# A hybrid block with 32 streamed experts: three experts kept on chip at the end, the first expert's bias loaded apart

## The chip, the cores and the metric

The kernel runs on one core of one Trainium2 chip. Its time is the device time of one execution in microseconds (us). Before the change it was 1566.69 us, the median of three runs (1562.38 to 1566.81). All data is float32.

## The reference

The block has one layer and 512 tokens of 1024 values. A mixer comes first (two kinds of recurrent heads); its result is added to x. Then comes the part that this change touches: a norm, a router, a mixture of 32 experts of which each token uses four, and a last norm.

```
h = modulate(rms_norm(x, norm_ffn), sh2, sc2)
logits = h @ w_router + b_router
top_logit, top_idx = top_k(logits, 4);  top_w = softmax(top_logit)
# for each expert e, the rows h[tok] of the tokens that chose it:
gu   = h[tok] @ w_gate_up[e] + b_gate_up[e]              # 1024 -> 2048
gate = minimum(gu[:, :1024], 7);  up = clip(gu[:, 1024:], -7, 7)
act  = (up + 1) * gate * sigmoid(1.702 * gate)
y    = act @ w_down[e] + b_down[e]                       # 1024 -> 1024
x    = x + g2 * sum over a token's four experts of top_w * y
out  = modulate(rms_norm(x, norm_final), sh_f, sc_f)
```

## The kernel before

The first 470 us are the mixer and the router. The router counts each expert's tokens and orders the experts on the chip by a table (ORDER gives, for a position in the program, the rank by number of tokens of the expert that is computed there; position 0 is always expert 0, the real one, since its weights are loaded before the order is known). In the following "expert n" is the n-th position.

**Weights.** An expert's weights are 12 MB: eight loads of 1 MB for gate_up ("gu", 128 rows of 2048 values each) and four for down ("wd"), all issued by SP. They go into 1 MB buffers, called `wst` in the profile, of which there are twenty; `fill` issues the next load (line 107) in a fixed list as soon as a buffer is free, so the loads follow each other as fast as buffers come free. `weights` (lines 1640 to 1649) writes that list: down of expert n-1 behind gate_up of n, and for the last two each expert's own down behind its gate_up.

**Rows.** Tokens go through an expert in groups of 32. UNITS_OF gives for every position how many groups are always computed and how many at most; the groups between stand under a branch on the expert's count. One group through one load is `up32`: four matmuls whose 32-column results lie side by side in U (groups 0 and 1) or E (groups 2 and 3). In the trace one float32 matmul leaves two records, so one group through one load is eight. The rows of an expert are gathered from the DRAM buffer xd (`gather`, POOL), transposed (`turn`, DVE), multiplied with gate_up, activated (`act`, DVE and ACT), multiplied with down, and written to a DRAM buffer yd (`send`, POOL). The bias enters U and E as a matmul of 8 rows (`add_bias`, line 1668) that opens the accumulation; `load_bias` brings it, POOL issuing the DMA.

**The first expert.** Its rows are not gathered: `first_rows` (line 1286) picks them by matmuls with a selection matrix P and ACT copies them (line 1288). In `up(0)` the first four loads serve groups 0 and 1 first; then every load serves the groups left, and is freed.

**The end.** Behind expert 29 stands `overflow`, a branch for counts that exceed the plan; in front of it all outstanding work is waited for. Then come experts 30 and 31, the two with the fewest tokens, of one group each. Expert 30's rows are kept on chip in Yb (line 1808). `fetch(k)` (lines 2062 and 2065) brings, for each token, the row of its k-th expert back from yd, in four indirect DMAs of 512 KB into the buffers yk, and DVE adds it to x: four fetches, 8 MB. `late_prep` builds selection matrices; `late_add` (lines 2094 and 2095) adds expert 30's kept rows by matmuls and DVE adds; `norm_all` takes the last norm; `late_rows` and `late_end` handle the tokens of expert 31, whose rows are computed last and written over the output by one scatter (line 2145).

The buffers of the end come from the same twenty (`last_slots`): yk takes two and other tables two, for which four are held in reserve; x and two more buffers of the kernel take four, and twelve carry the last loads.

Of the kernel before, what the change touches and what calls it, by code (L numbers as in the profile page):

```python
# [22 lines left out]
ORDER = [(0, 1, 1, 1, 0), (1, 5, 1, -1, 29), (5, 16, 5, 1, 1), (18, 19, 1, 1, 4), (21, 30, 2, 1, 5), (22, 29, 2, -1, 13), (6, 10, 1, -1, 25), (11, 15, 1, -1, 21), (16, 18, 1, -1, 17), (19, 21, 1, -1, 15), (30, 32, 1, -1, 31)]  # L23
# [4 lines left out]
UNITS_OF = [[(4, 4), (4, 6), (3, 4), (2, 3), (2, 2), (1, 2), (1, 1)][sum(r >= k for k in (1, 5, 10, 16, 26, 30))] for r in RANK]  # L28
# [651 lines left out]
class Mixer(Base):  # L680
# [598 lines left out]
    def first_rows(s, P, h):  # L1279

        p = s.b2([128, 4, 128], name="px")
        for k in range(4):
            for b in range(4):
                for q in range(4):
                    c = 256 * q + 32 * (4 * h + k)
                    s.nc.tensor.matmul(p[32 * q:32 * q + 32, k], s.h2s[b // 2][:, b % 2, c:c + 32], P[:, b], start=b == 0, stop=b == 3)
        for i, t in enumerate((s.xT[:, 0], s.xTx[:, 0:2])):
            s.nc.scalar.copy(t[:, :, 4 * h:4 * h + 4], p[:, :, 64 * i:64 * i + 64].rearrange("p k (u t) -> p u k t", u=2))
# [9 lines left out]
    def front(s):  # L1298
# [3 lines left out]
        c = s.fc  # L1302
        with s.tc.tile_pool(name="psf", bufs=1, space=PSUM) as ps:
# [47 lines left out]
            for b in range(4):  # L1351
                s.pump()
                ms = s.sm([128, 2], name="ms2")
                xT = []
                if b:
                    p = s.mix_mm(0, Y, lambda: xT.extend(s.x_T(b - 1, n) for n in range(2)))
                    pl = s.logits(xT)
                    del xT
                else:
                    Y1 = []  # L1360
                    p, p1 = s.mix_first(Y, lambda: Y1.extend(s.mix_T(1)))
                s.mix_add(b, 0, p, ms)
                if 0 < b < 3:
                    Y1 = s.mix_T(b + 1)
                p = s.mix_mm(1, Y) if b else p1
                if b == 3:
                    s.free(8)
                    s.fill()
                if b:
                    s.top4(b - 1, pl, prev)  # L1370
                s.mix_add(b, 1, p, ms)
                if b < 3:
                    Y = Y1
                else:
                    pl = s.logits([s.x_T(3, n) for n in range(2)])
                if b == 2:
                    s.free(2)
                if b == 0:
                    scale2()
                rs = s.norm2(ms)  # L1380
                if b % 2 == 0:
                    s.h2s.append(s.slot([128, 2, 1024], name="h2"))
                h2 = s.h2s[-1][:, b % 2]
                for n in range(2):
                    s.h2_rows(b, rs, h2, n, g if n or b < 3 else v)
                s.h2_out(b, h2, g)
                g.dma_start(s.xd[:, b], s.x[b])
                if b < 2:
                    s.heads_out(b + 2)
                if b == 1:  # L1390
                    s.free(2)
                    s.split_bias()
                if b < 3:
                    s.fill()
                prev = rs
            del Y, Y1, p
            s.top4(3, pl, rs)
# [20 lines left out]
class Block(Mixer):  # L1418
# [25 lines left out]
    def lists(s):  # L1444
# [18 lines left out]
        s.first_rows(s.P, 0)  # L1463
# [16 lines left out]
    def routing(s):  # L1480
# [19 lines left out]
        s.first_rows(s.P, 1)  # L1500
        del s.P
# [31 lines left out]
    def weights(s):  # L1533
# [56 lines left out]
        s.wl = c.tile([128, 4, 2], F32, name="wl")  # L1590
        v.tensor_copy(s.wl, s.pw[:, :, 30:32])
        late = s.sm([128, 4, 2], name="late")
        v.tensor_scalar(late, s.pos[:, :, 30:32], 32.0, None, op0=ALU.is_ge)
        v.tensor_mul(row[:, :, 30:32], row[:, :, 30:32], late)
        v.tensor_mul(s.pw[:, :, 30:32], s.pw[:, :, 30:32], late)
# [25 lines left out]
    def moe_weights(s):  # L1621
# [21 lines left out]
        for n in range(2, 30):  # L1643
            load_up(n)
            load_down(n - 1)
        load_down(29)
        for n in (30, 31):
            load_up(n)
            load_down(n)
# [16 lines left out]

    def add_bias(s, U, bias):
        s.nc.tensor.matmul(U, s.B8, bias, start=True, stop=False)  # L1668
# [68 lines left out]
    def up(s, e, mid=None):  # L1737
# [14 lines left out]
        if e == 0:  # L1752
            W = [s.get(("gu", 0, kk)) for kk in range(4)]
            for kk in range(4):
                for u in range(2):
                    s.up32(W[kk], xs[u], outs[u], kk)
            for kk in range(8):
                w = W[kk] if kk < 4 else s.get(("gu", 0, kk))
                for u in range(2 if kk < 4 else 0, 4):
                    s.up32(w, xs[u], outs[u], kk)  # L1760
                done()
                if kk == 3:
                    mid()
# [30 lines left out]
    def down_last(s, e):  # L1794
# [10 lines left out]
        if e == 30:  # L1805
# [47 lines left out]
    def moe(s):  # L1853
        nc = s.nc
        engs = [ET.PE, ET.Activation, ET.DVE]
        s.bias, s.c = {}, {}
        todo = s.weights()
        s.bias[0] = s.load_bias(0)
# [16 lines left out]
        for e in range(1, 31):  # L1875
            for u in range(2):
                s.gather(s.XG[:, (e + 1) % 2, u], s.idx[:, u, e + 1:e + 2])
            s.gather_more(e + 1)
            s.bias[e + 1] = s.load_bias(e + 1)
            if e == 28:  # L1880
                s.reserve = 3
            if e == 29:
# [3 lines left out]
            if e == 30:  # L1886
                s.last_slots()
                s.reserve = 0
                s.overflow()
                s.Yb = s.B1[:, 1]  # L1890
                nc.gpsimd.memset(s.Yb, 0.0)
                s.up(30)
                s.turn(31)
                s.down_last(30)
                for k in range(4):
                    s.fetch(k)
                s.late_prep()
                s.up(31)
                s.late_add()
                s.norm_all()  # L1900
                s.late_rows()
                break
# [6 lines left out]
            if e == 29:  # L1909
                s.down(29)  # L1910
                s.bias_down()
# [5 lines left out]
            if e == 3:  # L1917
                for u in range(2, 6):
                    s.index(u, s.y([128, 32], "y"))
        s.late_end(s.down_last(31))  # L1920
# [138 lines left out]
    def fetch(s, k):  # L2059

        for b in range(4):
            s.nc.gpsimd.indirect_dma_start(s.yk[b], None, s.yd[0:ROWA[30]],  # L2062
                                           bass.IndirectOffsetOnAxis(ap=s.rid[:, b, k:k + 1], axis=0))
        for b in range(4):
            s.nc.vector.scalar_tensor_tensor(s.x[b], s.yk[b], s.wk4[:, b, k:k + 1], s.x[b], op0=ALU.mult, op1=ALU.add)  # L2065

    def late_prep(s):
# [3 lines left out]
        tf, q5 = s.sm([128, 2], name="tf"), s.sm([128, 1], name="q5")  # L2071
        v.tensor_scalar(q5, s.qoff, -4096.0, None, op0=ALU.add)
        v.tensor_copy(tf, s.idx[:, 0, 30:32])
        v.tensor_scalar(tf, tf, q5, None, op0=ALU.subtract)
        v.tensor_scalar(s.PT, s.io5, tf[:, 0:1], None, op0=ALU.is_equal)  # L2075
# [3 lines left out]
        v.tensor_scalar(f, tf[:, 1:2], 4.0, None, op0=ALU.mult)  # L2079
# [8 lines left out]
    def late_add(s):  # L2088

        for b in range(4):  # L2090
            for n in range(2):
# [3 lines left out]
                s.nc.vector.scalar_tensor_tensor(s.x[b][:, ns], p, s.wl[:, b, 0:1], s.x[b][:, ns], op0=ALU.mult, op1=ALU.add)  # L2095
# [17 lines left out]
    def late_rows(s):  # L2113
# [8 lines left out]
        for b in range(4):  # L2122
            for j in range(4):
                te.matmul(w[32 * j:32 * j + 32, :], s.P1[:, b], s.wl[:, b, 1:2], start=b == 0, stop=b == 3)
# [60 lines left out]
```

## Time and profile before

| | |
|---|---|
| median of three runs | 1566.69 us (1562.38 to 1566.81) |
| the profiled execution | 1567.19 us |
| its span | 1565.6 us |
| PE busy | 1304.7 us, 83% |
| DVE, POOL, ACT busy | 549.2, 370.4, 180.5 us |
| read from HBM | 487.82 MB |
| mean rate of the span | 332 GB/s |

The profile is of one execution. Its span reaches from the first to the last instruction; the profiled execution's own time is 1.6 us longer. A line of the timeline is one instruction, or several alike that follow each other (x8), with its start, its length and, in brackets, how long its engine had been idle before and what released it. "SPq" is SP issuing DMAs. [...] The DMA share is the mean busy share of the core's 16 DMA engines; it can pass 1 by rounding.

### The profile page before, as it was taken

To read this page: it belongs to the slowest core of one execution; us is meant where nothing else is said; L and a number is where in the kernel's file an instruction comes from. 1 tells how busy PE (TensorE), PEld (TensorE's weight loads), DVE (VectorE), ACT (ScalarE), POOL (GpSimd) and SP (SyncE) were. 2 spreads that over 40 slices of the span, in tenths; PEclk is the share of its full clock that TensorE was granted. 3 is DMA by queue.
4 is the path that set the end of the run, shared out by engine and by line. 5 is a ranking of instruction groups with operands and counts; after the bars stand their busy time and mean duration, and the time that the engine had idled before them with its cause. 6 is when DMAs were issued, how large, how long until landed. Compare 5 with 4: busy or idle time off the path is not lost. (4 is left out here: it accounts for less than half of the span.)

```text
span 1565.6 us, 31529 instructions
## 1 busy us (share of the span) xinstructions
PE 1304.7 (83%) x13085; PEld 659.4 (42%) x13085; DVE 549.2 (35%) x1221; ACT 180.5 (12%) x366; POOL 370.4 (24%) x601
## 2 busy tenths in 40 slices
PE   5878978999978777899789978999898898887623
PEld 4656657967762322243224322434333342333201
DVE  6455552465753371332121212113111321112256
ACT  3433412144220000000000000000000000000001
POOL 2212234340221322021302130231222122212230
PEclk9989989969988886999999999999999999998757
DMA  9933535745186799999999999999999999999881
GB/s 303 331 114 135 206 131 156 293 183 165 44 346 268 297 415 415 417 417 417 417 419 417 417 418 417 417 413 417 414 416 411 414 416 412 415 410 393 323 361 56
DMA packets 135351, 518.40 MB, mean 331 GB/s; under 512 B 26454, under 2 KB 49642, under 8 KB 99338
## 3 DMA queue, kind: packets, MB, share of 16 engines
q1 hardware_dynamic: 108794, 465.68, 74.6%
q0 software_dynamic: 18960, 47.38, 7.9%
q10 hardware_dynamic: 7424, 2.89, 0.7%
q8 instruction: 126, 2.06, 0.5%
q14 instruction: 47, 0.39, 0.1%
HBM read 487.82 MB, written 32.51 MB: 332 GB/s over the span
## 5 line engine op out<-in xcount | busy, mean ns | idle before, releaser
L1674 PE MATMUL U<-wst,B 128*32 128x512 f32 x3712 | 449.6, 618 | 58.3 <-DMA wst<-in_w_gate_up 47.0
L1674 PEld LDWEIGHTS U<-wst,B 128*32 128x32 f32 x3712 | 117.8, 112 | 359.2 <-issue 245.3
L1696 PE MATMUL y<-wst,B 128*32 128x256 f32 x3712 | 221.6, 391 | 41.7 <-DMA wst<-in_w_down 28.6
L1706 POOL DMA_DIRECT2D yd<-ys x160 | 85.8, 542 | 604.2 <-DVE ys L1701 373.8
L1681 DVE TENSOR_SCALAR ag<-U 128x512 f32<-128x512 f32 (+1 forms) x32 | 20.5, 640 | 545.5 <-PE U L1674 519.1
L1696 PEld LDWEIGHTS y<-wst,B 128*32 128x32 f32 x3712 | 130.5, 112 | 144.6 <-DMA wst<-in_w_down 38.4
L1674 PE MATMUL E<-wst,B 128*32 128x512 f32 x1152 | 145.3, 614 | 9.4 <-DVE au L1683 9.4
L1682 ACT ACTIVATE as<-ag 128x512 f32<-128x512 f32 (+1 forms) x45 | 25.4, 564 | 972.4 <-DVE ag L1681 972.4
L532 POOL TENSOR_TENSOR lo<-wst,hi 128x1024 fp32r<-128x1024 f32 x30 | 74.8, 2512 | 156.3 <-ACT hi L531 154.5
L1520 POOL DMA_INDIRECT B<-xd,idx x62 | 65.9, 1063 | 109.8 <-DMA yd<-ys 41.3
L1701 DVE TENSOR_TENSOR ys<-y,g2j 128x256 f32<-128x256 f32 x72 | 30.5, 424 | 145.0 <-PE y L1696 132.1
L1674 PEld LDWEIGHTS E<-wst,B 128*32 128x32 f32 x1152 | 39.3, 113 | 98.9 <-issue 86.8
L1696 PE MATMUL y<-wst,h 128*32 128x256 f32 x1152 | 64.9, 380 | 1.8 <-DVE ys L1701 0.8
L573 PE MATMUL pu<-hi,hh 128*128 128x256 f32 x192 | 57.0, 297 | 6.0 <-DVE tmz L664 4.5
L574 PE MATMUL pu<-lo,hh 128*128 128x256 f32 x192 | 55.4, 289 | 0.0
L575 PE MATMUL pu<-hi,hl 128*128 128x256 f32 x192 | 55.1, 287 | 0.0
L628 DVE SCALAR_TENSOR_TENSOR cva<-cvt,tap,cva 128x511 f32<-128x511 f32 (+2 forms) x48 | 41.9, 879 | 24.6 <-ACT cva L625 23.3
L558 PE MATMUL pu<-hh,hi 128*128 128x512 f32 x96 | 41.5, 432 | 10.0 <-ACT cva L625 10.0
L1696 PEld LDWEIGHTS y<-wst,h 128*32 128x32 f32 x1152 | 36.9, 110 | 29.8 <-DVE ys L1701 7.3
L573 PEld LDWEIGHTS pu<-hi,hh 128*128 128x128 f32 x192 | 37.6, 196 | 10.8 <-DVE tmz L664 4.9
L1668 PE MATMUL U<-bias,B 8*128 8x512 f32 x58 | 23.0, 469 | 21.6 <-PEq L1719 8.4
L559 PE MATMUL pu<-hl,hi 128*128 128x512 f32 x96 | 39.3, 410 | 0.0
(545 smaller groups left out, 1524.3 us busy)
## 6 DMA issues: line engine op xcount, KB each, us to landing
wst<-in_w_gate_up SPq DMA_DIRECT2D x256, 1024.0 KB
wst<-in_w_down SPq DMA_DIRECT2D x128, 1024.0 KB
wst<-in_w_ada SPq DMA_DIRECT2D x24, 1024.0 KB
wst<-in_w_in SPq DMA_DIRECT2D x14, 1024.0 KB
yd<-zero POOLq DMA_DIRECT2D x7, 2048.0 KB, 22.7
wst<-in_w_ada_final SPq DMA_DIRECT2D x8, 1024.0 KB
yd<-ys POOLq DMA_DIRECT2D x124, 64.0 KB, 6.0
x<-in_x SPq DMA_DIRECT2D x8, 512.0 KB
```

Source lines behind the costliest of these rows:

```text
L532: (engs or (nc.gpsimd, nc.gpsimd))[n].tensor_sub(lo[:, a], w[:, a], hi[:, a].bitcast(F32))
L558: te.matmul(p[:, ct, :], hi[:, kk, cs], hx, start=kk == 0, stop=False)
L559: te.matmul(p[:, ct, :], hi[:, kk, cs], lx, start=False, stop=False)
L573: te.matmul(p[:, b, :], hx, hi[:, kk, :], start=kk == 0, stop=False)
L574: te.matmul(p[:, b, :], hx, lo[:, kk, :], start=False, stop=False)
L575: te.matmul(p[:, b, :], lx, hi[:, kk, :], start=False, stop=kk == 7)
L628: v.scalar_tensor_tensor(a[:, d:], th[:, :512 - d], w[j], a[:, d:], op0=ALU.mult, op1=ALU.add)
L1520: s.nc.gpsimd.indirect_dma_start(dst, None, s.xd4.rearrange("q t c -> (q t) c"), bass.IndirectOffsetOnAxis(ap=idx, axis=0), bounds_check=2 ...
L1674: s.nc.tensor.matmul(U[32 * j:32 * j + 32, :], x[:, kk, :], w[:, :, j, :], start=False, stop=kk == 7)
L1696: s.nc.tensor.matmul(y[32 * j:32 * j + 32, :], a[:, kt, :], W[:, kt % 2, 256 * j:256 * j + 256], start=start, stop=kt == 7)
L1701: s.nc.vector.tensor_mul(t, y, s.g2j)
L1706: s.nc.gpsimd.dma_start(rows.rearrange("(u t) c -> t u c", t=32)[:, :, 256 * j:256 * j + 256], t[32 * j:32 * j + 32])
```

## The change

Three positions are of the lightest kind, 29, 30 and 31 (one group each, where one more was possible at 29); the others move up by one position, with expert 4 of a smaller size. The branch `overflow` stands one expert sooner, behind expert 28. Experts 29 and 30 are both kept on chip and added by `late_add`; only 31 is still scattered. `fetch` is cut in two, DMA issue and adds, and the parts stand between the stages of the last three experts. For an expert of one group, one gather is issued in place of two.

At the start, `bias0` loads expert 0's bias as plain float32 into a place of its own, issued before the lists are made; `up(0)` puts all four groups through each load. `top4` of the third token block stands before that block's `h2_rows`, and `first_rows` is interrupted after two of its four column blocks so that the matmul of the order (pperm) comes between.

```diff
...
-UNITS_OF = [[(4, 4), (4, 6), (3, 4), (2, 3), (2, 2), (1, 2), (1, 1)][sum(r >= k for k in (1, 5, 10, 16, 26, 30))] for r in RANK]
+UNITS_OF = [[(4, 4), (4, 6), (3, 4), (2, 3), (2, 2), (1, 2), (1, 1)][sum(r >= k for k in (1, 5, 10, 16, 26, 29))] for r in RANK]
...
                 for q in range(4):
                     c = 256 * q + 32 * (4 * h + k)
                     s.nc.tensor.matmul(p[32 * q:32 * q + 32, k], s.h2s[b // 2][:, b % 2, c:c + 32], P[:, b], start=b == 0, stop=b == 3)
+            if k == 1:
+                yield
         for i, t in enumerate((s.xT[:, 0], s.xTx[:, 0:2])):
             s.nc.scalar.copy(t[:, :, 4 * h:4 * h + 4], p[:, :, 64 * i:64 * i + 64].rearrange("p k (u t) -> p u k t", u=2))
 
...
                 if b % 2 == 0:
                     s.h2s.append(s.slot([128, 2, 1024], name="h2"))
                 h2 = s.h2s[-1][:, b % 2]
+                if b == 3:
+                    s.top4(3, pl, rs)
                 for n in range(2):
                     s.h2_rows(b, rs, h2, n, g if n or b < 3 else v)
                 s.h2_out(b, h2, g)
...
                     s.fill()
                 prev = rs
             del Y, Y1, p
-            s.top4(3, pl, rs)
+            s.bias0()
             s.lists()
             s.free(2)
             s.fill()
...
         s.P = s.t2([128, 4, 128], name="P")
         for b in range(4):
             nc.vector.tensor_scalar(s.P[:, b], s.io, 1.0, pos[:, b:b + 1], op0=ALU.add, op1=ALU.is_equal)
-        s.first_rows(s.P, 0)
+        s.first = s.first_rows(s.P, 0)
+        next(s.first)
 
     def rounds(s, a, b):
...
         load_up(0)
         load_down(0)
         load_up(1)
-        for n in range(2, 30):
+        for n in range(2, 29):
             load_up(n)
             load_down(n - 1)
-        load_down(29)
-        for n in (30, 31):
+        load_down(28)
+        for n in (29, 30, 31):
             load_up(n)
             load_down(n)
 
...
         s.nc.gpsimd.dma_start(t.bitcast(F32), s.bgD[:, bass.ds(e, 1), :].rearrange("j o c -> j (o c)"))
         return t
 
+    def bias0(s):
+
+        t = s.B1[0:8, 1, 512:1024]
+        s.nc.gpsimd.dma_start(t, s.bgD[:, 0:1, :].rearrange("j o c -> j (o c)"))
+        s.bias = {0: t}
+
     def add_bias(s, U, bias):
-        s.nc.tensor.matmul(U, s.B8, bias, start=True, stop=False)
+        s.nc.tensor.matmul(U, s.B8 if bias.dtype == F32R else s.B8.bitcast(F32), bias, start=True, stop=False)
 
     def up32(s, W, x, U, kk):
 
...
             s.free(n)
             s.fill()
         if e == 0:
-            W = [s.get(("gu", 0, kk)) for kk in range(4)]
-            for kk in range(4):
-                for u in range(2):
-                    s.up32(W[kk], xs[u], outs[u], kk)
             for kk in range(8):
-                w = W[kk] if kk < 4 else s.get(("gu", 0, kk))
-                for u in range(2 if kk < 4 else 0, 4):
+                w = s.get(("gu", 0, kk))
+                for u in range(4):
                     s.up32(w, xs[u], outs[u], kk)
                 done()
                 if kk == 3:
...
                 w = None
                 s.free()
                 s.fill()
-        if e == 30:
+        if e < 31:
...
         s.up(0, mid)
         s.turn(1)
         s.c[1] = s.count(1, engs)
-        for e in range(1, 31):
-            for u in range(2):
-                s.gather(s.XG[:, (e + 1) % 2, u], s.idx[:, u, e + 1:e + 2])
-            s.gather_more(e + 1)
-            s.bias[e + 1] = s.load_bias(e + 1)
+
+        def ahead(e):
+            for u in range(min(UNITS_OF[e][1], 2)):
+                s.gather(s.XG[:, e % 2, u], s.idx[:, u, e:e + 1])
+            s.gather_more(e)
+            s.bias[e] = s.load_bias(e)
+        for e in range(1, 29):
+            ahead(e + 1)
+            if e == 27:
+                s.reserve = 3
             if e == 28:
-                s.reserve = 3
-            if e == 29:
                 s.load_xd()
                 s.bdown()
                 s.reserve = 4
-            if e == 30:
-                s.last_slots()
-                s.reserve = 0
-                s.overflow()
-                s.Yb = s.B1[:, 1]
-                nc.gpsimd.memset(s.Yb, 0.0)
-                s.up(30)
-                s.turn(31)
-                s.down_last(30)
-                for k in range(4):
-                    s.fetch(k)
-                s.late_prep()
-                s.up(31)
-                s.late_add()
-                s.norm_all()
-                s.late_rows()
-                break
             s.up(e)
             s.turn(e + 1)
             s.turn_more(e + 1)
             if UNITS_OF[e + 1][1] > UNITS_OF[e + 1][0]:
                 s.c[e + 1] = s.count(e + 1, engs)
             s.down(e - 1)
-            if e == 29:
-                s.down(29)
-                s.bias_down()
             next(todo, None)
             if e == 1:
                 s.rounds(8, 16)
...
             if e == 3:
                 for u in range(2, 6):
                     s.index(u, s.y([128, 32], "y"))
+        s.down(28)
+        s.bias_down()
+        ahead(30)
+        s.last_slots()
+        s.reserve = 0
+        s.overflow()
+        s.Yb = s.B1[:, 1]
+        nc.gpsimd.memset(s.Yb, 0.0)
+        got = [s.fetch(k) for k in range(4)]
+        next(got[0])
+        s.up(29)
+        s.turn(30)
+        ahead(31)
+        s.down_last(29)
+        s.late_prep()
+        s.late_add(29)
+        next(got[0], None)
+        next(got[1])
+        s.up(30)
+        s.turn(31)
+        next(got[1], None)
+        next(got[2])
+        s.down_last(30)
+        s.late_add(30)
+        next(got[2], None)
+        next(got[3])
+        s.up(31)
+        next(got[3], None)
+        s.norm_all()
+        s.late_rows()
         s.late_end(s.down_last(31))
 
     def overflow(s):
...
     def fetch(s, k):
 
         for b in range(4):
-            s.nc.gpsimd.indirect_dma_start(s.yk[b], None, s.yd[0:ROWA[30]],
+            s.nc.gpsimd.indirect_dma_start(s.yk[b], None, s.yd[0:ROWA[29]],
                                            bass.IndirectOffsetOnAxis(ap=s.rid[:, b, k:k + 1], axis=0))
+        yield
         for b in range(4):
             s.nc.vector.scalar_tensor_tensor(s.x[b], s.yk[b], s.wk4[:, b, k:k + 1], s.x[b], op0=ALU.mult, op1=ALU.add)
 
...
                 r = slice(32 * j, 32 * j + 32)
                 nc.gpsimd.tensor_copy(s.sj[r, h], s.B3[r, h, 256 * j:256 * j + 256])
 
-    def late_add(s):
-
+    def late_add(s, e):
+
+        s.nc.vector.tensor_scalar(s.PT, s.io5, s.tf[:, e - 29:e - 28], None, op0=ALU.is_equal)
         for b in range(4):
             for n in range(2):
                 p = s.y([128, 512], "y")
                 ns = slice(512 * n, 512 * n + 512)
                 s.nc.tensor.matmul(p, s.PT[:, 128 * b:128 * b + 128], s.Yb[:, ns], start=True, stop=True)
-                s.nc.vector.scalar_tensor_tensor(s.x[b][:, ns], p, s.wl[:, b, 0:1], s.x[b][:, ns], op0=ALU.mult, op1=ALU.add)
+                s.nc.vector.scalar_tensor_tensor(s.x[b][:, ns], p, s.wl[:, b, e - 29:e - 28], s.x[b][:, ns], op0=ALU.mult, op1=ALU.add)
 
     def norm_all(s):
 
...
```

What is left out of the diff: the table ORDER, the interleaving of `first_rows` in the lists, and widths that grow from two late experts to three (the weights `wl`, the row numbers `tf`, and the zeroing of the rows that are not in yd).

PE's row at the start of expert 0, before. U and E are the accumulators of groups 0, 1 and of 2, 3; the buffers B hold the rows and an 8-row selector; `wst` is a load.

```order
L1508 MATMUL pcnt<-sc,kcol 128x32
L1668 MATMUL U<-bias,B_188 128x512 x2
L1668 MATMUL E<-bias,B_188 128x512 x2
L1674 MATMUL U<-wst,B_3186 32x512 x32
L1674 MATMUL E<-wst,B_3186 32x512 x32
L1477 MATMUL y<-sc,L 32x32 x8
L1674 MATMUL U<-wst,B_3186 32x512 x8
L1674 MATMUL E<-wst,B_3186 32x512 x8
```

The same place in the changed kernel:

```order
L1515 MATMUL pcnt<-sc,kcol 128x32
L1681 MATMUL U<-B_3188,B_190 128x512 x2
L1681 MATMUL E<-B_3188,B_190 128x512 x2
L1687 MATMUL U<-wst,B_3188 32x512 x8
L1687 MATMUL E<-wst,B_3188 32x512 x8
L1687 MATMUL U<-wst,B_3188 32x512 x8
L1687 MATMUL E<-wst,B_3188 32x512 x8
```

The bias matmuls read a part of the buffer B1 in place of a bias tile, and 8 + 8 instructions of U and E now alternate from the first load on.

POOL behind the branch (line 1927), before: the kept rows' buffer is zeroed, then all sixteen DMAs of the four fetches (yk from yd), the copies for the last expert and the scatter of its rows.

```order
L1891 MEMSET B_3186 128x1024
L2062 DMA yk<-yd,rid 128x1024 x16
L2086 COPY last<-B_13567 32x256 x8
L2145 DMA out<-last,oidx 2048x256
L2181 UNCONDITIONAL_BRANCH
L2181 ISA
```

The same in the changed kernel, behind the same branch (line 1948 there):

```order
L1948 ISA
L1948 UNCONDITIONAL_BRANCH
L1918 MEMSET B_3188 128x1024
L2083 DMA yk<-yd,rid 128x1024 x4
L1527 DMA B_3189<-xd_215,idx 128x256
L1670 TENSOR_LOAD perm
L1670 ISA x2
L1671 ISA
L1671 DMA bias<-bgD 8x512
L2108 COPY last<-B_13336 32x256 x8
L2083 DMA yk<-yd,rid 128x1024 x12
L2168 DMA out<-last,oidx 2048x256
```

The gather of expert 31's rows (xd), its order number and its bias moved behind the branch and behind the first fetch; the copies stand ahead of the other three fetches.

DVE from expert 30's kept rows to the norm, before: `y,g2j` gives the kept rows, `yk,wk,x` are the adds of the fetches, `y,wl,x` those of the late expert, and `ssf` begins the norm.

```order
L1731 STREAM_TRANSPOSE B_3186<-B_3187 128x512
L1808 TENSOR_TENSOR B_3186<-y,g2j 32x256 x4
L2065 SCALAR_TENSOR_TENSOR x<-yk,wk_5940,x 128x1024 x16
L2072 TENSOR_SCALAR q_16468<-qoff 128x1
...
L2075 TENSOR_SCALAR last<-last,tf 128x512
L2077 TENSOR_SCALAR last<-io,pos 128x32 x4
...
L2082 CAST oidx<-of 128x1
L1681 TENSOR_SCALAR ag<-U 128x256
...
L1686 STREAM_TRANSPOSE B_3187<-au 128x256
L2095 SCALAR_TENSOR_TENSOR x<-y,wl,x 128x512 x8
L2105 TENSOR_SCALAR ssf<-ssf 128x4
```

The same in the changed kernel, from expert 29's kept rows on (line numbers of the changed kernel):

```order
L1744 STREAM_TRANSPOSE B_3188<-B_3189 128x512
L1817 TENSOR_TENSOR B_3188<-y,g2j 32x256 x4
...
L2112 TENSOR_SCALAR last<-last,tf 128x512
L2118 SCALAR_TENSOR_TENSOR x<-y,wl,x 128x512 x8
L2087 SCALAR_TENSOR_TENSOR x<-yk,wk_5915,x 128x1024 x4
...
L1744 STREAM_TRANSPOSE B_3188<-B_3189 128x512
L2087 SCALAR_TENSOR_TENSOR x<-yk,wk_5915,x 128x1024 x4
L1817 TENSOR_TENSOR B_3188<-y,g2j 32x256 x4
...
L2118 SCALAR_TENSOR_TENSOR x<-y,wl,x 128x512 x8
L2087 SCALAR_TENSOR_TENSOR x<-yk,wk_5915,x 128x1024 x4
...
L2087 SCALAR_TENSOR_TENSOR x<-yk,wk_5915,x 128x1024 x4
L2128 TENSOR_SCALAR ssf<-ssf 128x4
```

The sixteen adds of the fetches are cut into fours: one behind each late add, one ahead of expert 30's kept rows, one last, where the late adds stood before.

## Rows read from the trace of the kernel before

**Rows 1.** Page, part 2: granted clock and DMA share, tenths, 40 slices.
```profile
PEclk9989989969988886999999999999999999998757
...
DMA  9933535745186799999999999999999999999881
```

**Rows 2.** Windows: length; PE, PEld, DVE, ACT, POOL busy; PEclk; DMA share; GB/s.
```profile
466.00:472.00 6.00, 5.67 (x180) 4.93 (x172) 0.83 (x6) 1.24 (x4) 0.34 (x1) 1.00 0.64 220
472.00:480.00 8.00, 2.43 (x8) 1.36 (x12) 7.62 (x17) 0.05 (x1) 0.18 (x1) 0.70 1.01 424
480.00:492.00 12.00, 12.00 (x92) 3.05 (x88) 3.58 (x8) 0.00 (x0) 0.00 (x0) 0.77 0.04 16
516.00:526.00 10.00, 7.85 (x49) 1.98 (x53) 1.87 (x3) 0.00 (x0) 0.00 (x0) 0.65 0.11 19
600.00:1380.00 780.00, 701.54 (x7999) 272.04 (x8003) 171.18 (x341) 20.97 (x36) 165.71 (x236) 0.98 1.02 416
1458.00:1466.00 8.00, 7.73 (x52) 2.06 (x55) 0.00 (x0) 0.00 (x0) 0.95 (x1) 0.77 0.33 107
1466.00:1520.00 54.00, 21.36 (x147) 5.44 (x139) 20.99 (x23) 0.42 (x1) 15.47 (x17) 0.62 1.02 417
1522.00:1566.00 44.00, 15.58 (x152) 6.98 (x152) 28.60 (x63) 5.53 (x11) 4.82 (x8) 0.69 0.12 50
```

**Rows 3.** Timeline (start, us, engine, line, operation, wait): expert 0's start; last, L2041.
```profile
447.58 0.25 DVE L1241 SCALAR_TENSOR_TENSOR sc<-sc,rs,cvr 128x32 f32<-128x32 f32 x1
...
455.31 0.69 DVE L1277 TENSOR_TENSOR h<-hu,B 128x512 f32<-128x512 f32 x1
...
456.24 0.93 DVE L1241 SCALAR_TENSOR_TENSOR sc<-sc,rs,cvr 128x32 f32<-128x32 f32 x1
...
459.57 0.54 POOL L1387 DMA_DIRECT2D xd<-x  x1
...
471.40 0.65 ACT L1288 COPY B<-px 128x256 f32<-128x256 f32 x2 [3.42 <-PE px L1286]
...
471.66 0.52 POOL L1664 DMA_DIRECT2D bias<-bgD  x1 [10.59 <-PE px L1286]
...
477.57 1.19 PE L1668 MATMUL U<-bias,B 8*128 8x512 f32 x2 [5.89 <-DVE L L1470]
...
479.54 9.99 PE L1674 MATMUL U<-wst,B 128*32 128x512 f32 x64
...
489.36 7.04 PE L1674 MATMUL E<-wst,B 128*32 128x512 f32 x64
...
510.46 0.49 PE L1668 MATMUL U<-bias,B 8*128 8x512 f32 x1
...
517.96 6.13 PE L1674 MATMUL U<-wst,B 128*32 128x512 f32 x32 [7.01 <-DVE B L1731]
...
1441.07 10.96 PE L2041 MATMUL y<-bd,wT 32*128 32x512 f32 x16 [0.70 <-DVEq L1719]
```

**Rows 4.** Timeline of the end, from the restart of the loads on.
```profile
1464.52 1.29 SPq L107 DMA_DIRECT2D wst<-in_w_down  x2
...
1470.75 5.35 PE L1696 MATMUL y<-wst,B 128*32 128x256 f32 x64 [2.48 <-issue]
...
1472.12 1.00 POOL L2062 DMA_INDIRECT yk<-yd,rid  x1 [11.60 <-PE y L1696]
...
1489.39 1.93 PE L1674 MATMUL U<-wst,B 128*32 128x512 f32 x8 [1.81 <-DMA wst<-in_w_gate_up]
...
1526.16 3.75 PE L2094 MATMUL y<-B,last 128*128 128x512 f32 x4 [23.70 <-DVE last L2075]
...
1535.43 1.61 DVE L2095 SCALAR_TENSOR_TENSOR x<-y,wl,x 128x512 f32<-128x512 f32 x2 [0.36 <-PE y L2094]
```

**Rows 5.** Groups of lines, 1464 to 1566 us: busy, mean ns, idle before.
```profile
L2062 POOL DMA_INDIRECT yk<-yd,rid x16 | 15.1, 942 | 43.0 <-DVE x L2065 30.5 <-PE y L1696 11.6 <-issue 0.9
...
L2065 DVE SCALAR_TENSOR_TENSOR x<-yk,wk,x 128x1024 f32<-128x1024 f32 x16 | 20.7, 1300 | 25.9 <-DMA yk<-yd,rid 25.9
```

## What was predicted

> **What bounds the kernel now.** I read the slices of the span first: from the fifteenth slice of 39 us (548 us) to the last but two the DMA row stands at 9, with PE's granted clock near full [rows 1]. The windows say what that means: from 600 to 1380 us the DMA engines' share is 1.02 at 416 GB/s while PE is busy 701.54 of 780 us [rows 2]. One load of 1 MB (1.0486e6 bytes) at 416 GB/s takes 2.52 us, so an expert's twelve loads take 30.2 us, and nothing PE does faster in that stretch is worth anything. The time can only change where the stream of weights is not full. There are two such places, and the change touches both.
>
> The first is the start of the experts. From 466 to 472 us PE is busy 5.67 of 6 us at a granted clock of 1.00; from 472 to 480 it is busy 2.43 of 8 us and the clock is 0.70 on average, while the last loads of a full set of buffers land (share 1.01); from 480 to 492 the share is 0.04, because no buffer is free; from 516 to 526 it is 0.11 again [rows 2]. So up to 526 us PE's reading of expert 0 and 1 sets when buffers come free. The timeline shows the row: ACT has copied expert 0's inputs at 471.40 + 0.65 = 472.05, POOL issues the bias load at 471.66 (it had waited for PE's px), and PE's bias matmul begins only at 477.57 after 5.89 us of idling; weights follow from 479.54 to 510.46 [rows 3]. The profile names a DVE row as that wait's releaser; the bias DMA is issued in this very gap and is the only other input, so I hold it to be what came last.
>
> The second is the end. After the overflow branch the weights restart at 1464.52 [rows 4]. POOL's first row fetch stands at 1472.12 after 11.60 us of waiting for PE's y, for the fetch's buffers had held the last down matrices [rows 4]. From 1466 to 1520 the share is 1.02 at 417 GB/s, and from 1522 to 1566 it is 0.12 while DVE is busy 28.60 of 44 us [rows 2]. Hence the end is a full stream and then a chain of DVE, PE and ACT that nothing can hide. From the restart to the span's end it is 1565.6 - 1464.52 = 101.1 us.
>
> **Start.** What goes: the wait for the bias. It is now issued by POOL behind the two xd writes, the last of which stands at 459.57 [rows 3], so it has some 12 us to land where it took under 6 after its issue at 471.66. What is late next is ACT's copy, 472.05. The third top4 now stands ahead of block 3's h2 rows on DVE, which puts the two DVE instructions of that row (0.69 us for the one shown) behind it and so P later; less of it is waiting, so I take 0.8 us and PE's bias at 472.9, with bounds 472.1 (nothing) and 474.5 (both, and the sequence of eight small instructions of top4 between). What is added: the bias goes in as f32. The trace has no f32 matmul of 8 rows. Below, it is the present one, 1.97 us for four (477.57 to 479.54). Above, the b_down matmuls of L2041, 16 records for 8 matmuls in 10.96 us, 1.37 each at a lowered clock [rows 3], 5.5 for four. Four column-tiled 32-wide matmuls on f32 (one group through one load) take 7.04 / 8 = 0.88 us near full clock [rows 3]; I take that for each bias matmul, since it moves as many columns in as many passes, 3.5 in all. Weights then begin at 476.4 instead of 479.54.
>
> The order of the groups changes no work: 32 group-loads before and after. But the first 8 took 9.99 us, 1.25 each, the second 8 took 7.04 [rows 3], and the granted clock, 1.00 before the pause of 5.89 us, is 0.70 in its window and 0.77 in the next [rows 2]. With 0.9 us of pause I expect 0.88 throughout: 32 x 0.88 + 0.3 = 28.5, so expert 0's up ends at 504.9, against 510.46. The gain is 5.6, say 6 with the first buffers also free 11 us sooner (after 4 group-loads at about 480, not after 10 at 491). The bounds are 0 (the bias lands late, or the clock stays at half for as long as it did) and 9 (no f32 price, all of the idle time). Whether the early frees count by themselves: no, because the second gap, 516 to 526, would swallow it; it is filled by expert 1, whose first matmul waits 7.01 us for DVE's B, a chain that begins with the end of expert 0's up [rows 3]. It shifts as a whole, and that is the 6.
>
> **Middle.** The experts 20 to 28 of the new order are the former 21 to 29; the rest differ in order, not in bytes, and a light expert's one gather in place of two takes work from POOL, for which nothing waits. With the share at 1.02 this is worth 0 (bounds -2 and +2, by where a heavier expert falls). What is one expert sooner is the branch and the restart: 30.2 us.
>
> **End.** After the branch there were 2 + 8 + 4 = 14 loads and four fetches of 2 MB: 22 MB x 2.52 = 55.4 us, from 1466 to 1521, where the share is 1.02 (to 1520): the account closes [rows 2]. Now there are 26 loads and 8 MB, 34 MB, 85.7 us. The first fetch no longer waits for PE (its buffers held expert 28's down matrices, long read), so 0.86 MB (107 GB/s x 8 us, 1458 to 1466) plus more can move in the drained gap; I take 1 MB more than before. Then, in us from the restart: late_add(29) is 16 matmul records in pairs with 8 DVE adds, 1526.16 to 1535.43 + 1.61, 10.9 us [rows 4]; behind down_last(29), whose 64 records took 5.35 from 1470.75, i.e. to 11.6 [rows 4], and Yb and the late prep (4 us), it ends near 26.5. The four adds of fetch 0 follow (4 x 1.30 = 5.2 [rows 5]), and each frees a buffer for fetch 1. Beside gate_up loads a fetch gets a third of the stream (PE at 1489.39 waits 1.81 and works 1.93, so landings are 3.74 us apart [rows 4], instead of 2.52), beside down loads a half. So fetch 1 lands near 40, fetch 2 near 50, down_last(30) and late_add(30) end near 64, fetch 2's adds by 69, and fetch 3 is under way from 65. Expert 31's last gate_up lands after 22 loads, three fetches and some 1.2 MB of the fourth, less 1: 28.2 x 2.52 + 1.5 = 72.6. Then one group-load, 1.93, the activation, 2.48 (PE's pause ahead of 1470.75 [rows 4]), and four adds, 5.2, put the last x at 82.
>
> From the last late add (1537.04) to the end it was 28.5 us [rows 4], and this stays: norm, output, last expert's row scatter. Late_end's down needs the last load at 86, far inside. So the end takes 82 + 28.5 = 110.5 in place of 101.1: 9.4 of the 30.2 are given back, and the gain is 20.8. The two late adds and the late prep, which stood in the last stretch behind the stream, are now under it; that is where it comes from, and the bound of this gain is 30.2 (nothing given back) above and 14 below (each of fetches 1 to 3 taking 10 us behind the adds before it, late adds at 13.7: last x at 88.5).
>
> One thing in the rows speaks against it. Fetches 1 to 3 are now issued by POOL while DVE adds; formerly each issue (0.94 us on average, 16 of them [rows 5]) came behind its add, in a pause of DVE. Two engines side by side do hurt each other here: a DVE row of 0.25 us (447.58) took 0.93 at 456.24, with POOL computing beside it [rows 3]. [...] By the trace I charge nothing for the issues, for the stream has loads to move meanwhile. [...]
>
> **Sum.** 1565.6 - 6 - 20.8 = 1538.8, and the profiled execution stands 1567.19 - 1565.6 = 1.6 above its span: 1540.4, so 1540 us. That execution is 0.03% above the median of the runs, 1566.69, so nothing is corrected for it.
>
> **Rivals.**
> Fetch 3 is the last in (0.10). POOL's issues stick behind DVE or fetch 2's adds come late; fetch 3 then shares with the four last down loads at half, lands at 86, and the last x is at 87: 1545. For it: one buffer set serves four fetches in turn. Against it: 8 MB and the loads together fill only 86.
> The start gives nothing (0.10). The bias lands late behind two 512 KB writes on POOL's queue, or f32 bias matmuls at half clock eat the gain: 1546. For it: the clock did fall in that place. Against it: 12 us for a load that took under 6.
> The change does not do what it says (0.04): the stream is full all along, the end is a chain as long as before, and each expert-time won is paid back: 1565. Against it: the 44 us after the stream held late prep and late adds that are now ahead.
> Slower (0.04). After the branch twelve buffers form a ring: a load of expert 31 waits until PE has read the same matrix of expert 30, and PE's up(30) stands behind late_add(29), which goes step by step with DVE. The 14 loads without such a wait and fetch 0, less 1 MB, last until 15 x 2.52 + 1.5 = 39. If late_add(29) ends later, each us is lost to the stream. It decides once it loses over 26, an up(30) that begins at 65 in place of 26.5; with 30 lost it would be 1570. For it: three engines in one chain, and the DVE queue holds adds of rows that come late. Against it: the 10.9 us measured for these very adds.
> The forecast has the rest, 0.72, and in it 1530 to 1550 by the bounds of the start (-3 to +6) and of the end (-9 to +7) taken together.
>
> The range is 1530 to 1553: it takes in the first two rivals. What a measurement of this kernel can tell from no change is about 0.3%, 4.7 us. Faster by more is the forecast and the first two rivals and a little of the third, 0.93; within it 0.03; slower 0.04.
>
> **What would show it.** The first weight matmul near 476 with the clock at 1.00 behind it, and expert 0's up ending near 505; the branch and the restart 36 us sooner, near 1428; a first fetch that waits for no PE; the share at 1.0 for 85 us from there without a hole at up(30); and last x 82 us behind the restart, with 28.5 us to follow. A clock of 0.5 at expert 0, a stretch without loads between 30 and 60 us from the restart, or a fetch 3 landing behind the last gate_up by over 5 us would make it wrong.

## The result, and the profile after

The changed kernel took 1547.9 us, the median of six runs (1541.14 to 1554.43), beside 1564.86 for the kernel before (six runs, 1562.37 to 1566.81): a ratio of 0.9892, 95% interval 0.9863 to 0.992, some 17 us less. Forecast were 1540 and 27 us less. The profiled execution is the fastest of the six, 1541.14 us with a span of 1539.6.

Windows of that execution, with the columns of [rows 2] (PEclk is PE's granted clock as a share of full speed):

```profile
468.00:472.00 4.00, 4.00 (x22) 0.91 (x24) 3.79 (x10) 0.00 (x0) 0.00 (x0) 0.57 0.95 397
472.00:480.00 8.00, 8.00 (x80) 2.22 (x76) 4.20 (x9) 0.00 (x0) 0.00 (x0) 1.00 0.61 198
480.00:492.00 12.00, 12.00 (x132) 3.58 (x128) 0.41 (x2) 0.00 (x0) 5.96 (x31) 1.00 0.88 310
516.00:526.00 10.00, 9.82 (x188) 6.39 (x181) 2.58 (x6) 0.00 (x0) 2.21 (x4) 1.00 1.00 408
600.00:1340.00 740.00, 672.81 (x7697) 267.54 (x7693) 159.63 (x319) 19.30 (x33) 160.13 (x229) 0.99 1.02 412
1440.00:1500.00 60.00, 40.97 (x234) 12.70 (x226) 35.00 (x54) 0.42 (x1) 13.47 (x12) 0.80 1.02 416
1500.00:1539.00 39.00, 11.06 (x144) 4.16 (x144) 22.53 (x46) 5.52 (x11) 1.04 (x1) 0.62 0.51 204
```

All of expert 0 stands earlier in this execution (its first weights at 468.44, before at 479.54), so windows with the same figures do not hold the same work. At the first weights the clock is 0.57 from 468 to 472 and then 1.00; before, it was 0.77 from 480 to 492 [rows 2]. So it still fell, for a shorter time. Loads move from 480 on, where the share was 0.04 [rows 2]. In the middle the share is 1.02 as before, but at **412 GB/s in place of 416**; I had expected nothing there.

The timeline at expert 0's start (start, length, engine, line, operation, wait), answering to [rows 3]:

```profile
464.06 0.65 ACT L1291 COPY B<-px 128x256 f32<-128x256 f32 x2 [2.85 <-PE px L1287]
...
464.76 1.98 PE L1681 MATMUL U<-B,B 8*128 8x512 f32 x4 [0.43 <-ACT B L1291]
...
468.44 3.52 PE L1687 MATMUL U<-wst,B 128*32 128x512 f32 x16
...
498.03 0.49 PE L1681 MATMUL U<-bias,B 8*128 8x512 f32 x1
...
505.53 5.46 PE L1687 MATMUL U<-wst,B 128*32 128x512 f32 x32 [7.00 <-DVE B L1744]
```

PE's pause ahead of the bias matmul is 0.43 us and no longer 5.89; the eight bias records take 3.68 us to the first weights, and from these it is 29.6 us to the next expert's bias at 498.03 (30.9 before, from 479.54 to 510.46), where expert 0's up ends.

The timeline of the end, answering to [rows 4]; POOL's L2083 is a fetch's issue, DVE's L2087 its adds:

```profile
1423.97 1.02 POOL L2083 DMA_INDIRECT yk<-yd,rid  x1 [0.24 <-DMA B<-Rd]
...
1430.82 0.69 SPq L108 DMA_DIRECT2D wst<-in_w_down  x2
...
1444.82 9.40 PE L2117 MATMUL y<-B,last 128*128 128x512 f32 x16 [3.93 <-DVE last L2112]
...
1454.93 4.86 DVE L2087 SCALAR_TENSOR_TENSOR x<-yk,wk,x 128x1024 f32<-128x1024 f32 x4
...
1456.99 1.28 POOL L2083 DMA_INDIRECT yk<-yd,rid  x1 [18.91 <-DVE x L2087]
...
1458.58 2.02 POOL L2083 DMA_INDIRECT yk<-yd,rid  x1 [0.30 <-issue]
...
1460.91 0.94 POOL L2083 DMA_INDIRECT yk<-yd,rid  x1 [0.31 <-issue]
...
1492.31 4.86 DVE L2087 SCALAR_TENSOR_TENSOR x<-yk,wk,x 128x1024 f32<-128x1024 f32 x4
...
1493.85 1.74 POOL L2083 DMA_INDIRECT yk<-yd,rid  x1 [18.67 <-DVE x L2087]
1495.89 0.94 POOL L2083 DMA_INDIRECT yk<-yd,rid  x1 [0.31 <-issue]
...
1501.70 1.17 PE L1687 MATMUL U<-wst,B 128*32 128x512 f32 x8 [2.23 <-DMA wst<-in_w_gate_up]
...
1510.64 1.28 DVE L2087 SCALAR_TENSOR_TENSOR x<-yk,wk,x 128x1024 f32<-128x1024 f32 x1 [1.44 <-DMA yk<-yd,rid]
```

The first fetch goes out at 1423.97, behind no PE row. Loads restart at 1430.82; fetch 0's adds stand 24.1 us behind that (forecast 26.5), fetch 2's 61.5 (64), the last gate_up matmul 70.9 (72.6), and the last x is done at 1510.64 + 1.28, 81.1 behind (82). To the span's end it is another 27.7 (28.5). The end thus takes 108.8 us, forecast 110.5, before 101.1.

Two rows make the profiled execution look better than the change is. The router's first matmul, ahead of everything that the change touches, before and after:

```profile
406.28 0.65 PE L1228 MATMUL pl<-x2T,wr 128*32 128x128 f32 x16
```

```profile
400.43 0.64 PE L1229 MATMUL pl<-x2T,wr 128*32 128x128 f32 x16
```

What stands ahead of it took 5.9 us less in that execution. That is chance and no effect of the change: the changed kernel once more (e1) has the row at 405.66 and a span of 1548.3. So I measure from the router's row, or from the end of expert 0's up, in what follows.

### The profile page after: what moved, and what is told of

Its sections match the earlier page's. It is cut to its first block, busy times and chain, and to the rows that moved or that the text cites. A ratio compares the mean times of both kernels' runs of the same rounds, so it can differ in the third digit from the quotient of the medians.

```text
span 1539.6 us, 31537 instructions
## 1 busy us (share of the span) xinstructions
PE 1300.8 (84%) x13105; PEld 660.2 (43%) x13105; DVE 556.7 (36%) x1233; ACT 180.4 (12%) x366; POOL 364.8 (24%) x596
## 5 line engine op out<-in xcount | busy, mean ns | idle before, releaser
L1687 PE MATMUL U<-wst,B 128*32 128x512 f32 x3712 | 440.3, 608 | 45.0 <-DMA wst<-in_w_gate_up 26.3
L1709 PE MATMUL y<-wst,B 128*32 128x256 f32 x3712 | 225.3, 393 | 55.0 <-DMA wst<-in_w_down 38.0
L1527 POOL DMA_INDIRECT B<-xd,idx x59 | 62.2, 1054 | 106.8 <-DMA yd<-ys 34.4
L561 PE MATMUL pu<-hh,lo 128*128 128x512 f32 x96 | 38.3, 399 | 0.0
```

The source lines that it names most:

```text
L561: te.matmul(p[:, ct, :], lo[:, kk, cs], hx, start=False, stop=kk == 7)
L1527: s.nc.gpsimd.indirect_dma_start(dst, None, s.xd4.rearrange("q t c -> (q t) c"), bass.IndirectOffsetOnAxis(ap=idx, axis=0), bounds_check=2 ...
L1687: s.nc.tensor.matmul(U[32 * j:32 * j + 32, :], x[:, kk, :], w[:, :, j, :], start=False, stop=kk == 7)
L1709: s.nc.tensor.matmul(y[32 * j:32 * j + 32, :], a[:, kt, :], W[:, kt % 2, 256 * j:256 * j + 256], start=start, stop=kt == 7)
```

## Experiments

**The two parts apart.** e1 is the changed kernel once more. e2 is the kernel before with all edits of the start, e3 with the end and the table of experts alone, e4 with the two moves alone (shortened):

```diff
 # e4: kernel before, and
...
+                if b == 3:
+                    s.top4(3, pl, rs)          # ahead of h2_rows
...
-            s.top4(3, pl, rs)
...
+            if k == 1:
+                yield                          # first_rows in two parts
```

e1: 

> The changed kernel once more. Its six runs lie between 1541 and 1554 us, and the profiled one (the fastest) moves weights at 412 GB/s in the middle where the kernel before moved 416. Theory A (the stream of weights is slower in the changed kernel, by a varying amount): this profile comes out above 1545 us, and then its rate between 600 and 1340 us is below 412 GB/s, with the start (expert 0's up ending near 498 us) and the stretch from the restart to the end (108.8 us) unchanged. Theory B (the spread comes from TensorE's clock in the start or the end): the rate stays at 412 or above and the start or the end is longer by what the time is longer. A median of 1544 to 1551 under both.

e2: 

> Only the changes at the first expert: third top4 ahead of its rows, first_rows in two parts, the bias apart, four groups through each load; the end is the old one. If the 12.4 us that expert 0's up ended sooner reach the end: 1552 to 1553 us (gain 12). If only what I had forecast for the start does: 1559 (gain 6). If the stream's lower rate belongs to the new start: a rate near 412 GB/s in the middle and 1558 to 1563 us, the gain of the start lost in the middle. If it belongs to the new end or order of experts: rate 416 and 1552.

e3: 

> Only the end and the table of experts (three kept on chip, fetches moved up); the start is the old one. By the account of the prediction the end gains 30.2 less 9.4, so 1544 us; with the 7.7 us that the profile of the changed kernel shows given back, 1542. If the lower rate of the stream belongs to this part (the order of experts or where the buffers lie): rate 412 and some 9 us more, 1551 to 1553.

e4: 

> Of the start only two moves: the third top4 ahead of the h2 rows and first_rows in two parts; the bias as before, behind PE's px, and the old order of groups. PE's px began 7.1 us sooner in the changed kernel. If that alone made the start sooner: the bias matmul near 470.5, expert 0's up ending near 503.5, 7 us sooner, and 1558 us. If it only moves the wait (the bias load still lands at 477): no change, 1565.

Measured: e1 1547.89 us (in brackets the ratio to the runs of the kernel before beside it, with its 95% interval: 0.990, 0.988 to 0.992), e2 1561.62 (0.9989, 0.9975 to 1.0002), e3 1549.55 (0.9924, 0.9899 to 0.9949), e4 1565.82 (1.0016, 1.0003 to 1.003). e1 in the timeline (router, next bias, restart of the loads, the adds of fetch 2 and the last add of fetch 3):

```profile
405.66 0.64 PE L1229 MATMUL pl<-x2T,wr 128*32 128x128 f32 x16
...
504.69 0.49 PE L1681 MATMUL U<-bias,B 8*128 8x512 f32 x1
...
1436.08 1.48 SPq L108 DMA_DIRECT2D wst<-in_w_down  x2
...
1501.45 4.86 DVE L2087 SCALAR_TENSOR_TENSOR x<-yk,wk,x 128x1024 f32<-128x1024 f32 x4
...
1519.31 1.28 DVE L2087 SCALAR_TENSOR_TENSOR x<-yk,wk,x 128x1024 f32<-128x1024 f32 x1 [1.47 <-DMA yk<-yd,rid]
```

Its rate is again 412 GB/s, and from expert 0's up to the restart it needs 931.4 us, the first execution 932.8: the stream is not slower by a varying amount, as theory A of e1 had it. The 8.7 us by which e1's span is longer lie in the start and the end, where theory B had put them: 5.2 ahead of the router's row, 1.4 from there to the end of expert 0's up, 3.4 behind the restart (112.2 for 108.8), less 1.4 in the middle. That the clock made them is not shown. e2 moves 416, e3 412: the slower stream belongs to the new end or its table, and not to the start; e3's time lies between its two forecasts. And e2 shows that the start was worth little: of the 12.4 us that I took from the profile as its gain, 5.9 stood ahead of the router's row, and e2's whole gain in time is 1.7 us, with an interval that reaches to no change. In e4 the bias still lands late, as its second theory said:

```profile
461.99 2.62 DVE L1465 TENSOR_SCALAR P<-io,pos 128x128 f32<-128x128 f32 x4
...
478.76 1.19 PE L1673 MATMUL U<-bias,B 8*128 8x512 f32 x2 [5.72 <-DVE L L1474]
...
510.57 0.50 PE L1673 MATMUL U<-bias,B 8*128 8x512 f32 x1
```

P comes 1.4 us later behind the router's row (405.54) than before (461.28 behind 406.28), PE still waits 5.72 us, and nothing is gained.

**Where the buffers lie.** The built programs give the address of each of the twenty buffers within a partition: 8256 bytes apart, the first at 23552 in the kernel before, e2 and e4, and at 23776 in the changed kernel and e3. A scratch tile of the late experts (`late`, 32 bytes, 48 for three experts, with room for seven copies) stands ahead of them. 23552 is a multiple of 64, 23776 is 32 past one. e5 and e6 add 32 bytes, which move the twenty buffers and everything that is allocated behind them:

```diff
         s.cst = ctx.enter_context(tc.tile_pool(name="cst", bufs=1))
+        s.cst.tile([128, 8], F32, name="pad")
```

e5 (on the changed kernel): 

> The changed kernel with an unused tile of 32 bytes per partition ahead of the twenty buffers of the loads, and nothing else. In the kernel before, and in the two runs that kept its end, every buffer begins at a multiple of 64 bytes within a partition and the stream moves 416 GB/s; in the changed kernel and in the one with the new end alone the larger tables shift them all by 224 bytes, to 32 bytes past a multiple of 64, and it moves 412. Theory A (the place of the buffers slows each load by 1%): with 32 bytes more the rate is 416 again, and of some 890 us of full stream 8.6 come back: 1539 us. Theory B (the order of the experts or the new end slows it): 412 and 1548.

e6 (on the kernel before): 

> The kernel before with the same 32 bytes: every buffer 32 bytes past a multiple of 64. Theory A: 412 GB/s and 9 us slower, 1572 to 1573. Theory B: 416 GB/s and no change, 1564.

Measured: e5 1536.22 us (0.9825, 0.9812 to 0.9839), again in e9 1538.33 (0.9836, 0.9816 to 0.9856); e6 1574.38 (1.0063, 1.0049 to 1.0077). The page's row on the queue of the loads says it best: packets, MB, and the time that the packets took as a share of the span. Before, after, e5, e6:

```profile
span 1565.6 us, 31529 instructions
...
q1 hardware_dynamic: 108794, 465.68, 74.6%
```

```profile
span 1539.6 us, 31537 instructions
...
q1 hardware_dynamic: 108794, 465.68, 76.6%
```

```profile
span 1532.9 us, 31537 instructions
...
q1 hardware_dynamic: 108794, 465.68, 76.2%
```

```profile
span 1574.7 us, 31529 instructions
...
q1 hardware_dynamic: 108794, 465.68, 74.9%
```

The packets and bytes are the same in all four. Share by span, they took 1168 us before, 1179 after, 1168 in e5, 1179 in e6. 32 bytes of room, and nothing else, move the stream by 1%, in both kernels and in both directions. Over all runs the packets took 1166 to 1170 us with the buffers at multiples of 64 (seven runs) and 1177 to 1180 with them 32 past one (four). Theory B is out.

**How fine.** e10 makes every buffer begin at a multiple of 128 bytes, e11 every load at a multiple of 256; e9 is e5 once more, beside e10 (both cuts shortened; SHIFT lists the loads that go into a buffer at an odd multiple of 128):

```diff
 # e10, on e5 (room from scratch tiles that had seven copies each)
-s.late("mv", [128, 4, 4, 129])
+s.late("mv", [128, 4, 4, 130])        # buffers 8320 bytes apart
...
 # e11, on e10
-        t = s.slot(shape, name="wst")
+        o = 32 * (s.loads in SHIFT)   # buffers at an odd multiple of 128
+        t = s.slot([128, 2080], name="wst")[:, o:o + 2048]
```

e9: 

> The changed kernel with the 32 bytes, once more, as the measure for the next one on the same chip: 416 GB/s between 600 and 1340 us and 1536 us (1534 to 1539).

e10: 

> The same with every buffer at a multiple of 128 bytes (buffers 8320 bytes apart in place of 8256, first one at 23168; the room comes from small scratch tiles). With 8256 the buffers begin at 0, 64, 128 and 192 bytes past a multiple of 256 in turn, all at 416 GB/s on average. If 64 is the step that counts: 416 and no change, 1536. If a finer cut counts (a buffer at 64 past a multiple of 128 is slower than one at 0): 418 to 420 GB/s and 4 to 8 us faster, 1528 to 1532.

e11: 

> The kernel of e10 with each load placed 128 bytes further inside its buffer where the buffer begins at an odd multiple of 128: every load begins at a multiple of 256 bytes within a partition. The share of loads that begin off a multiple of 256 was 1 (412 GB/s), three quarters (416) and a little over half (419); if each such load costs the same, none of them gives some 426 GB/s, 1.6% of 890 us or 14 us, and 1516 us. If 128 is the step that counts: 419 and 1530.

Measured: e10 1529.85 us (0.978, 0.9762 to 0.9798), e11 1525.63 (0.974, 0.9716 to 0.9763; 1517.18 to 1531.37). The same rows, e10 and e11:

```profile
span 1527.0 us, 31537 instructions
...
q1 hardware_dynamic: 108794, 465.68, 76.0%
```

```profile
span 1529.8 us, 31537 instructions
...
q1 hardware_dynamic: 108794, 465.68, 75.6%
```

That is 1160.5 and 1156.5 us for the same packets. So 64 is not the step. That 128 is not either rests on one run of each: 4.0 us of packet time, where runs with loads in the same places differ by up to 3.7, 421 GB/s for 419, and intervals of the time that just touch. e11's 421 GB/s lie between the two forecasts, so loads off a multiple of 256 do not all cost the same. e11 has the lowest time of this case. Against its packets, loads in 64-byte places (e5) take 1.0% longer, those of e10 0.35%, those 32 past 64 (changed kernel) 2.0%.

**Which edit of the start.** e7 is e5 with the two moves of e4 taken back; e8 is the kernel before with only the bias apart (shortened):

```diff
 # e8
...
+            s.bias0()
             s.lists()
...
-        s.bias[0] = s.load_bias(0)
```

e7: 

> The changed kernel with the 32 bytes, and with the third top4 and first_rows back in their old places (the two moves that alone came out at a ratio of 1.0016). If they cost some 2.5 us and the bias and the order of the groups are what gains: 2 to 3 us faster than the changed kernel with the 32 bytes alone, about 1536 to 1537 under theory A. If the moves are needed once the bias is early (the bias's own landing is then no longer what PE waits for): 1 to 3 us slower, 1541.

e8: 

> The kernel before with expert 0's bias loaded apart as float32, and nothing else. By the traces PE's pause ahead of the bias matmul falls from 5.9 to about 0.5 us and the four matmuls take 3.8 in place of 2.0; weights then begin 3.6 us sooner. If that is what the start gains: expert 0's up ends 3.5 to 5 us sooner (less of it at a lowered clock) and the time is 1559 to 1560. If the order of the groups is needed for it: 1562 to 1564.

Measured: e7 1538.19 us (0.9828, 0.9814 to 0.9842), the same as e5; e8 1562.01 (0.999, 0.998 to 1.0). e8's bias records, and the next expert's bias, which stands where expert 0's up ends:

```profile
471.68 1.98 PE L1675 MATMUL U<-B,B 8*128 8x512 f32 x4 [0.43 <-ACT B L1288]
...
505.00 0.50 PE L1675 MATMUL U<-bias,B 8*128 8x512 f32 x1
```

PE's wait falls from 5.89 to 0.43 us with the bias load moved and DVE's rows left as they were: what PE had waited for was the bias, and not the DVE row that the profile names. From the router's row (406.18) expert 0's up ends after 98.8 us in e8; with the old start after 104.2, 102.2 and 102.1 (before, e6, e3), with the whole new start after 97.6, 99.0, 101.1 and 99.0 (after, e1, e2, e5; 98.7 to 99.3 in e9 to e11), and without the moves after 98.6 (e7). As far as these rows tell, the bias apart is the whole gain of the start, 3 to 5 us; the moves and the order of the groups add nothing that can be told apart. The times do not settle it: e8's 1562.01 lies where its second theory, by which the order is needed, had put it, and its gain of 0.1% or 1.6 us has an interval that reaches to no change; e7 is the same as e5, where its two theories had it faster or slower.

All runs in one table, in us, from their timelines; the packet time is share times span of the row shown above, which is rounded to some 0.8 us:

| kernel | loads begin at | rate GB/s | packet time | expert 0's up to restart | restart to end |
|---|---|---|---|---|---|
| before / e2 | multiple of 64 | 416 | 1168 / 1169 | 954.1 / 954.6 | 101.1 / 102.1 |
| e4 / e8 | multiple of 64 | 416 | 1166 / 1170 | 953.8 / 953.7 | 101.3 / 101.3 |
| e6 | 32 past | 412 | 1179 | 962.6 | 102.0 |
| after / e1 | 32 past | 412 | 1179 / 1180 | 932.8 / 931.4 | 108.8 / 112.2 |
| e3 | 32 past | 412 | 1177 | 931.6 | 110.0 |
| e5 / e9 | multiple of 64 | 416 | 1168 / 1170 | 921.8 / 922.6 | 109.2 / 107.6 |
| e7 | multiple of 64 | 416 | 1167 | 923.3 | 109.5 |
| e10 | multiple of 128 | 419 | 1160.5 | 915.9 | 107.3 |
| e11 | multiple of 256 | 421 | 1156.5 | 912.4 | 110.1 |

## Why the prediction was right, and where it was not

**The end: right.** With the buffers in places as good as before (e5 beside before), the branch and the restart come 32 us sooner than expert 0's up alone would make it, forecast 30.2, and the end takes 109.2, forecast 110.5. The chain of fetches, late adds and last loads came within 3 us at each of its marks. The ring of buffers did not stall it (share 1.02 from 1440 to 1500 in the profiled execution). But the path to the last x was not the forecast one, on which expert 31's last gate_up load decides. In all eight traces of the new end (after, e1, e3, e5, e7, e9, e10, e11) the last add waits for fetch 3 (1.44 us at 1510.64), as in the first rival, at a smaller price. That 82 was met so closely is in part luck, for the last gate_up matmul stood 1.7 us earlier. In e1 fetch 2's adds stood 65.4 us behind the restart instead of 61.5, three adds of fetch 3 waited 1.27 to 1.47 us each, and the last x was done at 84.5.

**The issues beside DVE's adds.** The issues at 1456.99, 1458.58 and 1493.85 took 1.28, 2.02 and 1.74 us, the one at 1460.91, behind the adds, 0.94. So POOL does lose time beside DVE, 2.2 us over the three; but the issue at 1495.89 took 0.94 though the adds ran to 1497.17. Why three were longer and this one was not is not shown. The prediction charged nothing for the issues, and the last x came at 81.1, forecast 82.

**The start: the mechanism was right, the size not.** The pause went (5.89 to 0.43), the price of float32 was 3.68 for 3.5 forecast. What failed is the clock term, "32 x 0.88 + 0.3 = 28.5": it took 29.6, so 1.3 us came back and not 2.4. The clock still fell, to 0.57, at the first two group-loads, which took 1.67 us each (468.44 to 471.78); the other thirty took 0.88. P stood 53.7 to 56.5 us behind the router's row with the moves (eight runs) and 53.1 to 55.0 without (five), 1.3 us later on average, forecast 0.8. Measured against the execution from which I forecast, the gain is near it: 104.2 less 99.0 is 5.2 us, forecast 5.6. But that execution's start was the longest of the three that kept it; against the others 3 us are left, and in the time 1.7, not clear of no change (e2).

**The middle: wrong.** "With the share at 1.02 this is worth 0 (bounds -2 and +2)" failed. It was mis-sized by 8.5 to 11.0 us (e6 against before 962.6 - 954.1, after against e5 932.8 - 921.8), for I took 2.52 us per load, measured in the kernel before, as given for the changed kernel too. It is one of the buffers' places, and the change moved these by making a small table wider. That accounts for nearly all that is missing: without it (e5, e9) the time is 25.7 to 27.4 us below before by the ratios, forecast 26.8. That the measured time lies inside the range all the same is owed to the range's width, which was drawn for other causes.

Why a load that begins off such a place takes longer is not shown here. That it follows the place is: the padding of e5 and e6 also moves what is allocated behind the buffers, but e11 moves only the loads within their buffers, and packet time and rate follow again, if only a little.

## What to carry to other kernels

When a kernel is bound by a stream of loads, look at the time of its packets for the same bytes (share times span) before and after any change, even one that does not touch them: a wider table can move every buffer. Put such buffers, and the loads in them, at multiples of 256 bytes within a partition; here that took the changed kernel from 1547.9 to 1525.6 us (ratios 0.9892 and 0.974), more than the change itself gained; multiples of 128 gave most of it. And measure a stage from a mark just ahead of it: what stands earlier varied by 5 us between two executions of one program.

## What was not expected of the hardware

The rate at a DMA share of 1.02 stood at four levels, 412, 416, 419 and 421 GB/s, for the same packets and bytes, by where loads begin in a partition (32 past a multiple of 64; at multiples of 64, 128, 256); the last two are from one run each. Two executions of the same program had the router's first matmul at 400.43 and 405.66 us; why is not shown.
